# A hybrid attention, gated-recurrence and feed-forward layer in float32: score pairs issued together, the mark for values set later, the first gates and gated head fetched earlier

## The chip, the cores and the metric

The kernel runs on one core of a Trainium2 chip. The metric is the device time of one execution in microseconds, the median of several runs; a profiled execution of the same program gives the trace that is read here.

## The reference

One layer over 256 tokens of width 2048, all in float32:

```python
parts = x @ w_in                      # 9 parts of 1024 for three attention groups, then gq, gk, gv, gr, g_low, m_a, m_b
o, lse = _dilated_group(q, k, v, ...) # per group: windowed attention, 8 heads of 128, with a bias by distance
ya = softmax-over-groups(lse) * o, summed, @ w_proj_a
o  = _gla(gq, gk, gv, log_a)          # gated linear attention, 4 heads of 256 x 512, chunks of 64 tokens
yb = (normed(o) * silu(gr)) @ w_proj_b
y  = (sigmoid(m_a) * ya + sigmoid(m_b) * yb) @ w_out
x1 = layernorm(a * x + y)
f  = (silu(conv(x1 @ w_gate)) * (x1 @ w_up)) @ w_down      # 5632 wide, a 3-tap convolution over tokens
out = layernorm(a * x1 + f)
```

## The kernel before

**Numbers.** Each float32 operand is split into two parts (`split`, L138): ScalarE (ACT) copies it to a rounded high part `whi`, and VectorE (DVE) subtracts that from the original to leave a low part `wlo`. A product takes the matmuls high by high, high by low and low by high. Weights come as pieces of 128x1024 (512 KB), loaded by the SyncE queue into tiles `raw` or `quarter`, and each piece costs one split on ACT and one on DVE.

**Work in the first half.** The projections of x come in two forms. A *tile* (`b16`, L239) makes 128 columns with 32 matmuls; 64 of these make gq, gk and the attention's q and k. A *unit* (`seven`, L323) makes two 512-column blocks with seven products instead of eight (Strassen's scheme): its steps p1, p5, p6, p7, p3, p2, p4 appear in the trace as matmuls into the banks A, D, B, E, D, A, E, 24 matmuls each. Sums of x are kept in four resident tiles `comb`; sums of weights are made by DVE (L350) or by an accumulating DMA of GpSimd (POOL, L353). Ten units make v, gv, gr and most of m_a and m_b. `of_units` lists their steps, and the loop at L778 puts 56 tiles between them evenly.

**Side work.** Attention and the recurrence are cut into short closures in two lists, `side` and `slow`. `pump` (L188) runs one or two of them before every step and every tile. A closure may carry a mark and is held until the mark is in `passed`: the fetch of v (L515) waits for `values`, which the last `v` unit sets, and a stage of the recurrence waits for `gv`. Setting a mark (L754 to L756) was a step of its own in the list of units. Score matmuls (L470) of both token halves write into one PSUM bank, and DVE moves each half out (L472).

**Order.** The tracing order only sets priorities. A scheduler that builds the program decides, engine by engine, in which order the instructions stand, and `tc.issue_after(x)` keeps an instruction behind `x` on its engine. Each engine then works strictly in its order: an instruction that waits holds everything behind it, and that includes a DMA that stands in the ACT or POOL order and waits for its source.

**Around the middle.** After the units, two plain chunks of m_b (`m_t`, L798) are made, the early pool of SBUF tiles is closed and a late pool opens (L804). Then come four chunks `yp` (w_proj_a, 48 matmuls each, L899) and four chunks `pb` (w_proj_b, 96 each, L909). A chunk's gate is a spilled block of m, fetched again (tiles `m`, L876), put through a sigmoid (L884) and multiplied by DVE (L886). Beside the `yp` chunks the four heads of the recurrence's output are gated: `gated_get` fetches gr and o (L844), `gated_mul` takes the sigmoid and two products (L851 to L854), and `gated_turn` transposes the result on TensorE (`pt<-ident,sg`, L817; 8 transposes a head) and moves it out on ACT and DVE (`ob`, L824 and L825). The `pb` chunks read `ob`.

Of the kernel before, what the change touches and what calls it, by code (L numbers as in the profile page):

```python
# [11 lines left out]
F32 = mybir.dt.float32  # L12
# [5 lines left out]
P = 128  # L18
# [42 lines left out]
def hybrid_layer(ctx: ExitStack, tc: tile.TileContext, wp, xt, wgl, gw, par, relb, onehot, rows, xk, out):  # L61
# [73 lines left out]
    nc.gpsimd.memset(eps, EPS)  # L135


    def split(hi, lo, src):  # L138
        nc.scalar.activation(hi, src, AF.Copy)  # L139
        nc.vector.tensor_tensor(lo, src, hi.bitcast(F32), op=ALU.subtract)  # L140

    home = ["raw", 4]
# [306 lines left out]
    def attend(h, qk):  # L449
# [11 lines left out]
        def scores(g):  # L461
            def f():
                if not g:
                    st["s"] = blk("s0")[:, :384], big("s1", (768,))
                q, k = qk[g][:, :S], qk[g][:, S:]
                ps = bank("ps")
                for t in range(2):
                    n = (t + 1) * P
                    pt = ps[:, t * P : t * P + n]
                    nc.tensor.matmul(pt, q[:, t * P : (t + 1) * P], k[:, :n], start=True, stop=True)  # L470
                    s = st["s"][t][:, g * n : (g + 1) * n]
                    nc.vector.scalar_tensor_tensor(s, pt, scale, st["T"][:, g, S - n :], op0=ALU.mult, op1=ALU.add)  # L472
            return f
# [277 lines left out]
    def by_unit(name, n, sink, mark=None):  # L751
        for u in range(n):
            yield from seven(name, X, comb, AT[name, u], sink(u))
            if not u:  # L754
                yield lambda: passed.add("low")
        yield lambda: passed.add(mark)  # L756

    tiles = of_tiles()
    with tc.issue_after(loaded.ins):
# [12 lines left out]
        yield from by_unit("gr", 2, lambda u: to(GR, u))  # L772
        yield from by_unit("m", 3, lambda u: to(M[u // 2], u % 2))

    units = list(of_units())
    rest = list(tiles)
    done = 0
    for n, step in enumerate(units):  # L778
        pump()
        step()  # L780
        while done < (n + 1) * len(rest) / len(units):
            pump(2 if len(side) > 12 else 1)
            rest[done]()
            done += 1
# [8 lines left out]
        return f  # L793

    side.extend(ya_parts(h) for h in range(NH))
    yop = lambda kc: YA2[kc // 4][:, kc % 4]
    for n in range(2):
        pss = a_chunk("m", xop, 16, AT["mb"] + 8 * n, 3)  # L798
# [48 lines left out]
    def gated_mul(h):  # L847
        def f():
            sgs = [blk("sg") for _ in range(2)]
            for sg, (x, o) in zip(sgs, got[h]):  # L850
                nc.scalar.activation(sg, x, AF.Sigmoid)  # L851
                nc.vector.tensor_tensor(x, x, o, op=ALU.mult)
            for sg, (x, o) in zip(sgs, got[h]):
                nc.vector.tensor_tensor(sg, sg, x, op=ALU.mult)  # L854
            got[h] = sgs
        return f
# [6 lines left out]
    def both(*fs):  # L863
        def f():
            for g in fs:
                g()
        return f
# [28 lines left out]
    ya = []  # L896
    for n in range(4):
# [432 lines left out]
```

## Time and profile before

| | |
|---|---|
| median of 3 runs | 1888.59 us (1885.82 to 1895.8) |
| the profiled execution's own time | 1893.98 us |
| its span, first to last instruction | 1892.3 us |
| TensorE (PE) busy | 1824.9 us, 96% of the span, 8974 matmuls |
| weight loads (PEld) / DVE / ACT / POOL busy | 1523.2 / 1446.7 / 1088.3 / 243.5 us |
| granted TensorE clock, mean of the span | 0.989 |
| DMA | 478.53 MB, mean 253 GB/s |

A matmul's row in the trace lasts longer than its turn on the engine, because matmuls overlap: 24 matmuls of 128x512 that follow each other without a wait take 5.47 us, so one takes 0.228 us. PE's idle time is therefore the sum of the gaps that the view of waits names; it does not hold what a lower granted clock costs.

### The profile page before, as it was taken

To read this page: it belongs to the slowest core of one execution; us is meant where nothing else is said; L and a number is where in the kernel's file an instruction comes from. 1 tells how busy PE (TensorE), PEld (TensorE's weight loads), DVE (VectorE), ACT (ScalarE), POOL (GpSimd) and SP (SyncE) were. 2 spreads that over 40 slices of the span, in tenths; PEclk is the share of its full clock that TensorE was granted. 3 is DMA by queue.
4 is the path that set the end of the run, shared out by engine and by line. 5 is a ranking of instruction groups with operands and counts; after the bars stand their busy time and mean duration, and the time that the engine had idled before them with its cause. 6 is when DMAs were issued, how large, how long until landed. Compare 5 with 4: busy or idle time off the path is not lost.

```text
span 1892.3 us, 25421 instructions
## 1 busy us (share of the span) xinstructions
PE 1824.9 (96%) x8974; PEld 1523.2 (80%) x8974; DVE 1446.7 (76%) x1715; ACT 1088.3 (58%) x1400; POOL 243.5 (13%) x361
## 2 busy tenths in 40 slices
PE   8999998999999999999999999999999999999996
PEld 6877887788888888788778887888888888888785
DVE  6967997788797978865755556796597787877878
ACT  6655775565666666655654435665565556556553
POOL 0112111111111211111300001001011110110211
PEclk9999999999999999999999998999999999999998
DMA  8898987979889897896866518669679769779682
GB/s 303 278 304 228 305 276 218 326 211 306 256 260 338 216 310 241 258 338 229 301 235 205 189 60 321 210 166 321 225 206 341 241 202 338 222 229 341 190 276 95
DMA packets 145419, 478.53 MB, mean 253 GB/s; under 512 B 17649, under 2 KB 27916, under 8 KB 145292
## 3 DMA queue, kind: packets, MB, share of 16 engines
q1 hardware_dynamic: 96764, 345.09, 51.2%
q0 software_dynamic: 34416, 118.62, 25.5%
q10 hardware_dynamic: 14112, 13.21, 2.2%
q8 instruction: 70, 1.15, 0.2%
q14 instruction: 57, 0.47, 0.1%
HBM read 382.41 MB, written 32.67 MB: 219 GB/s over the span
## 4 chain that ended last, share of the span: by engine, by line
PE 69%; DMA 10%; DVE 9%; issue 4%; ACT 2%; POOL 1%; ACTq 0%; DVEq 0%; SPq 0%; POOLq 0%
PE qk L230 7%; DVE wlo L140 4%; PE wd_t L267 4%; PE wd_t L266 4%; PE wd_t L268 4%; PE qk L232 4%; PE fu L230 3%; PE fguE L337 3%; DMA quarter<-in_wp 3%; PE fg L230 3%; PE fguA L337 2%; DMA raw<-in_wp 2%; PE fguD L337 2%; PE mE L337 2%; PE pb_t L267 2%
## 5 line engine op out<-in xcount | busy, mean ns | idle before, releaser
L140 DVE TENSOR_TENSOR wlo<-quarter,whi 128x1024 fp32r<-128x1024 f32 x484 | 579.4, 1221 | 207.4 <-issue 61.1
L139 ACT ACTIVATE whi<-quarter 128x1024 fp32r<-128x1024 f32 x484 | 505.4, 1058 | 300.4 <-DVE quarter L350 58.5
L139 ACT ACTIVATE whi<-raw 128x1024 fp32r<-128x1024 f32 (+1 forms) x346 | 359.6, 1053 | 257.7 <-DMA raw<-in_wp 119.8
L140 DVE TENSOR_TENSOR wlo<-raw,whi 128x1024 fp32r<-128x1024 f32 (+1 forms) x346 | 414.4, 1215 | 112.8 <-ACT whi L139 49.6
L230 PE MATMUL qk<-x,whi 128*128 128x512 f32 x768 | 192.2, 399 | 0.0
L353 POOL DMA_DIRECT2D quarter<-quarter x120 | 105.6, 903 | 601.9 <-DMA quarter<-in_wp 157.1
L230 PEld LDWEIGHTS qk<-x,whi 128*128 128x128 f32 x768 | 141.9, 188 | 29.4 <-issue 1.4
L350 DVE TENSOR_TENSOR quarter<-quarter,quarter 128x1024 f32<-128x1024 f32 x120 | 143.2, 1219 | 0.3
L267 PE MATMUL wd_t<-wlo,h 128*128 128x512 f32 x352 | 137.6, 391 | 0.6 <-DVE wlo L140 0.6
L266 PE MATMUL wd_t<-whi,h 128*128 128x512 f32 x352 | 137.3, 392 | 0.0
L268 PE MATMUL wd_t<-whi,h 128*128 128x512 f32 x352 | 136.6, 389 | 0.0
L232 PEld LDWEIGHTS qk<-x,wlo 128*128 128x128 f32 x768 | 98.5, 191 | 7.5 <-DVE wlo L140 3.7
L232 PE MATMUL qk<-x,wlo 128*128 128x256 f32 x768 | 100.1, 283 | 3.3 <-DVE wlo L140 3.3
L230 PE MATMUL fu<-x,whi 128*128 128x512 f32 x368 | 88.0, 391 | 0.5 <-DVE gc L1004 0.4
L230 PE MATMUL fg<-x,whi 128*128 128x512 f32 x352 | 84.0, 390 | 0.0
L230 PEld LDWEIGHTS fu<-x,whi 128*128 128x128 f32 x368 | 68.2, 188 | 15.3 <-PE pt L1045 1.2
L267 PEld LDWEIGHTS wd_t<-wlo,h 128*128 128x128 f32 x352 | 66.2, 188 | 14.1 <-DVE wlo L140 1.3
L268 PEld LDWEIGHTS wd_t<-whi,h 128*128 128x128 f32 x352 | 66.1, 188 | 14.0 <-DVE h L140 0.3
L266 PEld LDWEIGHTS wd_t<-whi,h 128*128 128x128 f32 x352 | 66.0, 188 | 13.4 <-ACT h L139 0.3
L230 PEld LDWEIGHTS fg<-x,whi 128*128 128x128 f32 x352 | 65.5, 188 | 13.3
L230 PE MATMUL gqk<-x,whi 128*128 128x512 f32 x256 | 65.7, 409 | 4.4 <-ACT whi L139 3.6
L230 PEld LDWEIGHTS gqk<-x,whi 128*128 128x128 f32 x256 | 50.2, 200 | 17.8 <-ACT whi L139 7.4
(366 smaller groups left out, 3202.9 us busy)
## 6 DMA issues: line engine op xcount, KB each, us to landing
raw<-in_wp SPq DMA_DIRECT2D x342, 512.0 KB, 5.2
quarter<-in_wp SPq DMA_DIRECT2D x304, 512.0 KB, 6.9
quarter<-quarter POOLq DMA_DIRECT2D x120, 512.0 KB, 9.0
af<-acc POOLq DMA_DIRECT2D x32, 256.0 KB, 6.5
acc<-af POOLq DMA_DIRECT2D x28, 256.0 KB, 5.7
sp<-c POOLq DMA_DIRECT2D x14, 256.0 KB, 8.3
bias<-bvd ACTq DMA_DIRECT2D x32, 96.0 KB, 5.1
v<-vs ACTq DMA_DIRECT2D x24, 128.0 KB, 7.4
```

Of the source, the lines that this page charges most:

```text
L139: nc.scalar.activation(hi, src, AF.Copy)
L140: nc.vector.tensor_tensor(lo, src, hi.bitcast(F32), op=ALU.subtract)
L230: nc.tensor.matmul(ps, parts(kc)[0], opnd(kc), start=(kc == 0), stop=False)
L232: nc.tensor.matmul(ps[:, S:], parts(kc)[1], opnd(kc)[:, :S], start=False, stop=(kc == nk - 1))
L266: nc.tensor.matmul(ps, xh, hi, start=first, stop=False)
L267: nc.tensor.matmul(ps, xh, lo, start=False, stop=False)
L268: nc.tensor.matmul(ps, xl, hi, start=False, stop=last)
L337: nc.tensor.matmul(ps, a(kc)[which], w[:, k * 512 : (k + 1) * 512], start=(first and w is hi and which == 0 and kc == 0), stop=(w is lo an ...
L350: tt(a, a, b, op=ALU.add)
L353: nc.gpsimd.dma_start(a, b, accum_op=ALU.add)
```

## The change

It has five parts.

1. `scores` issues the matmuls of both token halves first and the two DVE instructions after them.
2. Setting a mark is no longer a step among the units. The mark is noted for two steps later and set there before `pump`. With that four empty steps leave the list (78 to 74), so the tiles and the side work shift against the units.
3. Two resident tiles `G01` and `GO` (of the size of a `comb` tile, from the same pool of 8) are fetched on the POOL queue while the `m_t` chunks are traced: the four blocks of the gates of chunks 0 and 1, and gr and o of head 0. Before, all of these were fetched from the late pool.
4. The sigmoids of gates and gated heads are kept behind the newest weight split on ACT.
5. The list of side work for the `yp` chunks starts with `mul(0)` and puts one of `mul` and `turn` at each of the eight places.

```diff
     def split(hi, lo, src):
-        nc.scalar.activation(hi, src, AF.Copy)
+        newest[:] = [nc.scalar.activation(hi, src, AF.Copy)]
...
                 for t in range(2):
                     n = (t + 1) * P
-                    pt = ps[:, t * P : t * P + n]
-                    nc.tensor.matmul(pt, q[:, t * P : (t + 1) * P], k[:, :n], start=True, stop=True)
+                    pts.append(ps[:, t * P : t * P + n])
+                    nc.tensor.matmul(pts[t], q[:, t * P : (t + 1) * P], k[:, :n], start=True, stop=True)
+                for t, pt in enumerate(pts):
+                    n = (t + 1) * P
                     s = st["s"][t][:, g * n : (g + 1) * n]
                     nc.vector.scalar_tensor_tensor(s, pt, scale, st["T"][:, g, S - n :], op0=ALU.mult, op1=ALU.add)
...
-        yield lambda: passed.add(mark)
+        yield mark
...
-    units = list(of_units())
+    units, marks = [], {}
+    for step in of_units():
+        if callable(step):
+            units.append(step)
+        else:
+            marks[len(units) + 2] = step
...
     for n, step in enumerate(units):
+        passed.add(marks.get(n))
         pump()
         step()
...
+    G01, GO = res("g01", F32), res("go", F32)
+
+    def first_fetches(t):
+        def f():
+            for n in range(2):
+                nc.gpsimd.dma_start(G01[:, 2 * n + t], M[0][n][t])
+            nc.gpsimd.dma_start(GO[:, 2 * t], GR[0][t])
+            nc.gpsimd.dma_start(GO[:, 2 * t + 1], O[0][t])
+        return f
+
+    slow.extend([first_fetches(0), first_fetches(1)])
...
-                nc.scalar.activation(sg, x, AF.Sigmoid)
+                with tc.issue_after(newest[0].ins):
+                    nc.scalar.activation(sg, x, AF.Sigmoid)
...
-                new = [fetch("m", M[br][n][t]) for t in range(2)]
+                if not br and n < 2:
+                    new = [G01[:, 2 * n + t] for t in range(2)]
+                else:
+                    new = [fetch("m", M[br][n][t]) for t in range(2)]
...
-            last_gate[:] = [nc.scalar.activation(x, x, AF.Sigmoid)]
+            with tc.issue_after(newest[0].ins):
+                last_gate[:] = [nc.scalar.activation(x, x, AF.Sigmoid)]
...
-    gated_get(0)()
+    got[0] = [[GO[:, 2 * t], GO[:, 2 * t + 1]] for t in range(2)]
     gated_get(1)()
...
     side.extend([
-        lambda: None, mul(0), both(turn(0), get(2)), mul(1),
-        both(turn(1), get(3)), mul(2), both(turn(2), mul(3)), turn(3),
+        mul(0), turn(0), both(mul(1), get(2)), turn(1),
+        both(mul(2), get(3)), turn(2), mul(3), turn(3),
     ])
```

The built program shows where this moves instructions. Line numbers of the change lie a little higher than those of before (L817 is L841, L139 and L140 are L141 and L142, L353 is L355, L518 is L523); numbers behind a name tell one buffer from another.

On PE, in the `yp` chunks, the transposes of head 0 stood so:

```order
L266 MATMUL yp_t_1089_8263<-whi_8330,ya_7729 128x512
L267 MATMUL yp_t_1089_8263<-wlo_8331,ya_7729 128x512
L268 MATMUL yp_t_1089_8263<-whi_8330,ya_7729 128x512
L817 MATMUL pt_8302<-ident,sg_8247 128x128
L817 MATMUL pt_8311<-ident,sg_8247 128x128
L266 MATMUL yp_t_1090_8264<-whi_8330,ya_7729 128x512
L817 MATMUL pt_8302<-ident,sg_8248 128x128
```

and now:

```order
L269 MATMUL yp_t_1074_8168<-wlo_8234,ya_7727 128x512
L270 MATMUL yp_t_1074_8168<-whi_8233,ya_7727 128x512
L268 MATMUL yp_t_1086_8276<-whi_8280,ya_7726 128x512
L841 MATMUL pt_8250<-ident,sg_8205 128x128
L841 MATMUL pt_8259<-ident,sg_8205 128x128
L269 MATMUL yp_t_1086_8276<-wlo_8281,ya_7726 128x512
L270 MATMUL yp_t_1086_8276<-whi_8280,ya_7726 128x512
L841 MATMUL pt_8250<-ident,sg_8206 128x128
```

They moved from behind 75 `yp` matmuls to behind 49. The four heads stood behind 75, 120, 168 and 192 `yp` matmuls and now stand behind 49, 96, 144 and 192.

On POOL, at the last unit of m, the four sums that p4 needs (`quarter<-quarter`, the second four) followed the first four at once:

```order
L353 DMA quarter_7130<-quarter_7243 128x1024
L353 DMA quarter_7132<-quarter_7245 128x1024
L353 DMA quarter_7134<-quarter_7247 128x1024
L353 DMA quarter_7077<-quarter_7515 128x1024
L353 DMA quarter_7079<-quarter_7517 128x1024
L353 DMA quarter_7081<-quarter_7519 128x1024
L353 DMA quarter_7083<-quarter_7521 128x1024
L112 DMA sp_7405<-c_963_7402 128x512
```

and now (`g` is G01, `go` is GO, `os` a spilled block of o):

```order
L355 DMA quarter_7166<-quarter_7301 128x1024
L814 DMA g_1007_7728<-sp_6168 128x512
...
L814 DMA g_1007_7728<-sp_5933 128x512
L112 DMA os_7222<-o_7216 128x512
L112 DMA os_7234<-o_7228 128x512
L815 DMA go_7729<-sp_4635 128x512
L816 DMA go_7729<-os_4516 128x512
L355 DMA quarter_7054<-quarter_7570 128x1024
L355 DMA quarter_7056<-quarter_7572 128x1024
```

Six fetches and two stores came between them. The first `g` reuses a `comb` tile that p7 of this unit reads, and the first `go` one that p3 reads.

On ACT, at the end of the third unit of v, the third fetch of v for head 0 stood so:

```order
L139 ACTIVATE whi_2769<-raw_2767 128x1024
L518 DMA v_2645<-vs_0_110 128x2x128
L258 ACTIVATE pa_2695<-qk_2661 128x256
L139 ACTIVATE whi_2825<-quarter_2704 128x1024
L496 ACTIVATE pT_2702<-ppt_2698 128x384
```

and now stands so:

```order
L141 ACTIVATE whi_2753<-raw_2751 128x1024
L523 DMA v_2895<-vs_0_110 128x2x128
L260 ACTIVATE pa_2691<-qk_2657 128x256
L141 ACTIVATE whi_2806<-quarter_2694 128x1024
L141 ACTIVATE whi_2816<-quarter_2696 128x1024
```

The fetch kept its place between the splits of a tile and the move `pa` of the tile before; what left the place is the attention's `pT` behind it. From the end of the `pb` chunks on, every engine's order is the same as before.

More of the change, by code (lines that the diff above doesn't have):

```diff
@@ L135, in hybrid_layer @@
     nc.gpsimd.memset(eps, EPS)
+    newest = []
     def split(hi, lo, src):
-        nc.scalar.activation(hi, src, AF.Copy)
+        newest[:] = [nc.scalar.activation(hi, src, AF.Copy)]
         nc.vector.tensor_tensor(lo, src, hi.bitcast(F32), op=ALU.subtract)
@@ L466, in f @@
                 ps = bank("ps")
+                pts = []
                 for t in range(2):
                     n = (t + 1) * P
-                    pt = ps[:, t * P : t * P + n]
-                    nc.tensor.matmul(pt, q[:, t * P : (t + 1) * P], k[:, :n], start=True, stop=True)
+                    pts.append(ps[:, t * P : t * P + n])
+                    nc.tensor.matmul(pts[t], q[:, t * P : (t + 1) * P], k[:, :n], start=True, stop=True)
+                for t, pt in enumerate(pts):
+                    n = (t + 1) * P
                     s = st["s"][t][:, g * n : (g + 1) * n]
```

## The prediction

> **What bounds the kernel now.** I read the page first, then PE's waits, then the stretches and the chain of waits where those waits lie.
>
> ```profile
> span 1892.3 us, 25421 instructions
> PE 1824.9 (96%) x8974; PEld 1523.2 (80%) x8974; DVE 1446.7 (76%) x1715; ACT 1088.3 (58%) x1400; POOL 243.5 (13%) x361
> ```
>
> PE is busy in 96% of the span and the change removes no matmul, so it can win only what PE loses: 1892.3 - 1824.9 = 67 us of idle time, and clock. The view of waits for PE says whom it waits for (total us, times, longest):
>
> ```profile
> PE pt L817 <- DVE ob L825: 4.6, 2, 3.0
> ...
> PE ps L470 <- DVE s L472: 3.7, 2, 2.6
> ...
> PE qk L232 <- DVE wlo L140: 3.3, 1, 3.3
> ...
> PE vD L337 <- DVE wlo L140: 3.0, 2, 2.6
> PE vE L337 <- ACT whi L139: 2.9, 2, 1.8
> PE pt L817 <- issue: 2.3, 1, 2.3
> PE vB L337 <- DVE wlo L140: 2.0, 1, 2.0
> PE mB L337 <- DVE wlo L140: 1.7, 2, 1.1
> ...
> PE gvB L337 <- DVE wlo L140: 1.5, 1, 1.5
> ...
> PE gvD L337 <- DVE wlo L140: 1.3, 1, 1.3
> PE yp_t L267 <- DVE wlo L140: 1.1, 1, 1.1
> ...
> PE pt L817 <- DVE sg L854: 1.1, 2, 0.9
> ```
>
> Nothing is large: the kernel loses its time in some thirty waits of 1 to 4 us. Three places belong to this change: the transposes of the gated heads with the yp row, the scores (ps), and the qk, gvD and gvB waits near 304 us, which a fetch of v causes.
>
> **The gated heads** (parts 3 to 5). The stretches of 10 us show busy times of PE, PEld, DVE, ACT and POOL, then the granted clock; the first is a full one. The chain of waits goes on behind the last gap:
>
> ```profile
> 895.00:905.00 10.00, 10.00 (x46) 8.28 (x45) 7.18 (x11) 6.53 (x12) 3.94 (x8) 1.00 0.84 269
> 905.00:915.00 10.00, 7.69 (x35) 5.97 (x33) 5.04 (x6) 4.68 (x5) 5.13 (x11) 1.00 1.01 383
> 925.00:935.00 10.00, 7.82 (x37) 5.94 (x37) 9.84 (x14) 6.48 (x12) 2.04 (x4) 1.00 0.84 258
> 945.00:955.00 10.00, 5.39 (x22) 4.17 (x21) 6.85 (x11) 6.16 (x11) 2.13 (x4) 0.81 0.83 290
> ...
> 953.17 0.43 PE pb_t L266
> ...
> 957.87 0.39 PE pb_t L268
> 958.26 0.24 PE pb_t L266
> ```
>
> Idle PE: 2.3 + 2.2 + 4.6 = 9.1 us, which the three pt rows and the yp row also make (4.6 + 2.3 + 1.1 + 1.1). Behind the last gap the clock falls to 0.81 and twelve matmuls, 953.17 to 958.26, take 5.1 us; at the later 0.228 us apiece they take 2.7. That is 2.4 us more, so this place costs 11.5 us.
>
> The Trainium skill, "TensorE: Matmul & The Clock Gate", Part 1: The HAM clock gate, says that the clock halves after an idle window of some 3.4 us and recovers after one busy window. The rows agree: gaps of 2.3 and 2.2 us left the clock at 1.00, 4.6 us did not, and 0.43 us is about twice 0.228. By the page alone the return would be half a window, 1.7 us (an estimate from the page), and the sum below 0.7 us smaller.
>
> Why PE waits there: the fetches of gr and o.
>
> ```profile
> 903.44 0.54 POOL L117 DMA_DIRECT2D gr<-sp  x1 [5.33 <-PE yp_t L268]
> ...
> 903.20 1.23 DVE L140 TENSOR_TENSOR wlo<-raw,whi 128x1024 fp32r<-128x1024 f32 x1 [0.77 <-issue]
> ...
> 910.70 0.69 DVE L852 TENSOR_TENSOR gr<-gr,o 128x512 f32<-128x512 f32 x1 [0.84 <-DMA o<-os]
> 913.08 0.69 DVE L852 TENSOR_TENSOR gr<-gr,o 128x512 f32<-128x512 f32 x1 [1.69 <-DMA o<-os]
> 913.69 1.29 DVE L854 TENSOR_TENSOR sg<-sg,gr 128x512 f32<-128x512 f32 x2
> ```
>
> The first can be issued at 903.4, the fourth block is used at 913.1, and DVE, nearly idle before that, then has all four heads' work in 30 us (9.84 of 10 busy in 925 to 935). In the change head 0's data and two chunks' gates lie ready, and DVE begins with head 0 after its fourth wlo. From the rows: that wlo ends at 903.2 + 1.2 = 904.4; two products gr by o (0.65 each, half of 1.29) and two with sg end at 907.0, the first pair's half at 906.4. PE reaches the transposes after 48 to 49 matmuls of 0.228 us from 895.0, at 906.1: 0.4 to 1 us late. Head 1's four blocks take the places in the queue that head 0's have in these rows, so DVE ends head 1 by about 915.1 (913.1 + 0.7 + 1.3), and the wlo behind it at 916.3; PE needs that wlo (85 `yp` matmuls and eight transposes of about 0.13 us after 895.0, plus the 0.5 us above) at 916 and head 1's transposes at 918.5. Heads 2 and 3 have 11 us each, and DVE's work for one chunk is four wlo, four products, two gates and four ob: 4.9 + 2.6 + 1.4 + 1.8 = 10.7 us. That just fits, so I keep 1.5 us of waits and no clock loss: 11.5 - 1.5 = **10.0 us won**. Bounds: 11.5 if nothing waits, 0 if DVE runs late again. The sigmoids moved behind weight splits cost ACT nothing new (58% busy); without that slack they delay a split by 0.6 us each.
>
> One step does go ahead of work on this path: ACT's table load and the first two sigmoids now stand around the last head's `ya`, whose way through DRAM and back ends here:
>
> ```profile
> 900.87 0.42 DVE L140 TENSOR_TENSOR ya<-yaf,ya 128x256 fp32r<-128x256 f32 x1
> ...
> 907.80 1.28 ACT L851 ACT_TABLE_LOAD   x1
> ```
>
> The load and one sigmoid (1.9 us) put that last split from 901.3 to 903.2 at most; PE wants it after 42 matmuls, at 904.6. Hidden by those matmuls: **0 us**, and under 2 us if the store lands that much later.
>
> **The moved fetches.** All eight are 256 KB on POOL's queue, six of them ahead of the second four weight sums of the last m unit. `go` waits until p3 has read its tile, and POOL holds the sums behind it.
>
> ```profile
> 815.87 5.47 PE mD L337 x24
> ...
> 833.70 5.49 PE mE L337 x24
> ...
> 816.83 0.86 POOL L353 DMA_DIRECT2D quarter<-quarter  x1 [2.63 <-ACT pa L258]
> ...
> quarter<-quarter POOLq DMA_DIRECT2D x120, 512.0 KB, 9.0
> ...
> DMA to landing us min/median/max: 4.6/9.0/20.2
> ```
>
> Before, the last of the four sums was issued at 816.8 and p4 (the last mE) began at 833.7. Now p3 (mD) ends at 821.3, two `go` issues take 1.1 us, and the four sums are issued from 822.4 to 825.1; with the median of 9.0 us they land from 831.4 to 834.1, and a split takes 2.3 us more. In the change a second qk tile of 5.5 us stands between p3 and p4, so p4 starts near 838 and wants its fourth piece 4.1 us later. First piece 4 us early, fourth 5 to 6 us: **0 us**, hidden by the two tiles. If the sum lands after the longest 20.2 us (700 to 817 us), the fourth is ready at 847.6 and PE stops for 5.5 us, and 8 with the clock's 2.4: the upper bound.
>
> **The scores** (part 1). The ps row is the second half's matmul waiting for DVE to read the first half out of the same bank. Issued together, it no longer waits: **3.7 us won**. DVE's instruction for the first half starts some 0.3 us later, beside other matmuls. Bounds: 0 to 3.7.
>
> **The later mark** (part 2).
>
> ```profile
> 290.92 0.72 POOL L563 DMA_DIRECT2D vs<-u  x1
> ...
> 300.55 0.53 ACTq L518 DMA_DIRECT2D v<-vs  x1
> 301.13 0.38 ACT L258 ACTIVATE pa<-qk 128x256 f32<-128x256 f32 x1 [9.28 <-PE qk L230]
> ...
> 301.54 0.42 DVE L259 TENSOR_TENSOR qk<-qk,pa 128x256 f32<-128x256 f32 x1 [7.77 <-ACT pa L258]
> 301.88 1.22 DVE L350 TENSOR_TENSOR quarter<-quarter,quarter 128x1024 f32<-128x1024 f32 x1
> 303.02 2.35 DVE L140 TENSOR_TENSOR wlo<-raw,whi 128x1024 fp32r<-128x1024 f32 x2
> ```
>
> The fetch of v stands in ACT's order and waits from 291.9 to 300.5 for the store of v to land. Behind it wait `pa`, on DVE the add after it, and the wlo that the qk row waits for; gvD and gvB pay the rest: 3.3 + 1.3 + 1.5 = 6.1 us. The later mark should remove that. The order says it does not: the scheduler pulls the fetch forward to the same place, ahead of the same `pa`. Only one weight sum of 1.2 us (L350) now stands behind the two wlo instead of ahead. **1.2 us won**, with bounds 0 and 6.1. The four steps that leave the list were empty and cost nothing; they shift side work. The vD, vE, vB and mB rows, 9.6 us, are splits that come late for such reasons: I count no change, and let them vary by half either way.
>
> **Sum.** 10.0 + 0 + 3.7 + 1.2 = 14.9 us. The profiled execution took 1893.98, so 1879.1 as it would be profiled; it lies 5.4 us above the median of the runs, 1888.59, and I take the win from that: 1888.59 - 14.9 = 1873.7, **1874 us**, 0.8% faster. About 0.5% (9.4 us) is what a measurement of this kernel can tell from no change, so the borders are 1879.1 and 1898.0.
>
> **Rivals.**
>
> *A, DVE becomes the bound of the yp stage.* For: 10.7 us of DVE work in a chunk of 10.9, and head 1's wlo within 0.3 us of its need. Against: DVE stood at 5.04 of 10 just before. If half of the 9.1 us returns and with it the clock's 2.4, 4.6 + 2.4 - 1.5 = 5.5 us come off the win: 1879 to 1880.
>
> *B, the queue of POOL.* The sums behind `go` land late, as priced, up to 8 us: 1874 to 1882.
>
> *C, the mark does what it says.* ACT is not held at 291.9, since the store lands earlier or the fetch finds it landed. For: the median landing of such stores is shorter than these 9.6 us. Against: the same place in the order. 6.1 - 1.2 = 4.9 us more: 1869.
>
> *D, slower.* One mechanism: with the empty steps gone, tiles and units meet in another order between 57 and 890 us, and the split of a piece stands behind another in-order wait on ACT or DVE (as near 291.9), so the waits of vD, vE, vB, mB and qk multiply. These rows, with gvB and gvD, hold 15.7 us. It eats the win when they double (1889) and is slower beyond 0.5% from about 2.6 times (+24 us, 1898). For: half of the order on all engines differs. Against: units and tiles have the same amount of loads and splits as before, and no row of the page shows an engine full there.
>
> **How the numbers follow.** The forecast (1866 to 1879) has 0.47, C 0.10, A 0.18, B 0.10, D 0.15. Faster by over 0.5%: nearly all of the forecast (0.44), C, a third of A and B's small stalls (0.05): 0.64, from which I take 0.04 because several small waits must all go. Slower: two thirds of D, 0.10. Same: the rest, 0.30. Range: from 1864 (the forecast with all upper bounds, 1.5 + 4.9 + 3 more than the sum) to 1892 (D where the rows double, and 3); the forecast's own is 1866 to 1879.
>
> **What would show it.** PE's waits on L470 gone; no wait above 1 us at the transposes of `sg` and a clock of 1.00 in every stretch of the yp and the first pb chunk (right), or DVE above 9.5 of 10 with waits on wlo there (A). Beside the last mE of the m units a wait for wlo with `quarter<-quarter` behind it (B). On ACT a fetch of v with some 9 us of nothing behind a store, once, near 290 (right about the mark), or none (C). The sum of PE's vD, vE, vB, mB and qk waits above 25 us would mean D. I am wrong in mechanism if the time falls and the yp stage still shows its 9.1 us.

## The result and the profile after

The changed kernel takes 1875.94 us (median of 4 runs, 1874.49 to 1877.26), the kernel before 1888.24 us (median of 4 beside it, 1885.82 to 1895.8). The ratio is 0.9928 with a 95% interval of 0.9899 to 0.9957: 0.7% faster. The forecast was 1874 us and faster. The sum came out; two of its terms were far off in opposite directions, as the runs below show, so that the sum came out is luck.

The page of the profiled execution (own time 1875.52 us) begins so, the span first, then each engine's busy time, share and instructions:

```profile
span 1873.8 us, 25413 instructions
PE 1819.0 (97%) x8974; PEld 1522.2 (81%) x8974; DVE 1443.2 (77%) x1715; ACT 1088.6 (58%) x1400; POOL 240.3 (13%) x361
```

The span is 18.5 us shorter than in the profile of before, 6 us more than the medians differ: that execution of before was 5.4 us above its median. PE's waits, those that answer to the rows quoted in the prediction (total us, times, longest):

```profile
PE vD L339 <- DVE wlo L142: 4.7, 2, 4.0
...
PE qk L234 <- DVE wlo L142: 3.3, 1, 3.3
PE vB L339 <- DVE wlo L142: 3.1, 2, 2.5
...
PE gvD L339 <- DVE wlo L142: 2.8, 2, 1.5
PE yp_t L269 <- DVE wlo L142: 2.4, 2, 1.2
...
PE pt L841 <- issue: 1.7, 1, 1.7
...
PE mB L339 <- DVE wlo L142: 0.5, 1, 0.5
```

The ps row is gone, as forecast, and the transposes of the heads wait 1.7 us in place of 8.0. But the rows vE (2.9) and gvB (1.5) are gone too, and mB fell from 1.7 to 0.5, none of which was forecast; the rows vD, vB and gvD rose by 1.1 to 1.7 each, and the yp row from 1.1 to 2.4.

The yp stage of the changed kernel in stretches of 10 us (columns as in the prediction: busy time of PE, PEld, DVE, ACT, POOL, granted clock, share of the DMA engines, GB/s):

```profile
893.00:903.00 10.00, 8.32 (x41) 6.70 (x40) 6.44 (x11) 6.50 (x12) 6.44 (x13) 1.00 0.81 304
903.00:913.00 10.00, 8.77 (x42) 6.97 (x42) 9.99 (x15) 2.51 (x4) 4.23 (x8) 1.00 0.99 358
913.00:923.00 10.00, 8.85 (x39) 7.01 (x38) 7.34 (x11) 7.55 (x12) 0.78 (x2) 1.00 0.77 263
```

The clock stays at 1.00, but PE still loses 1.7 + 1.2 + 1.2 = 4.1 us, and DVE is full for one stretch.

The instruction behind the fetch of v on ACT (start, duration, engine, instruction, idle time ahead of it and what ended that):

```profile
299.33 0.38 ACT L260 ACTIVATE pa<-qk 128x256 f32<-128x256 f32 x1 [8.67 <-DMA vs<-u]
```

The fetch, issued at 298.75 us, holds ACT for 8.7 us, as it did before (9.28 us).

Two stretches carry the rest of this text. One is the units and tiles with the plain gate chunks, from the first vA matmul to the first yp matmul; the other is the yp stage, from there to the first pb matmul. Both contain the same work in all kernels below. In the profiles of before and after, the first one reads:

```profile
57.27:895.00 837.73, 814.94 (x4076) 680.32 (x4075) 673.72 (x744) 510.64 (x644) 120.35 (x162) 1.00 0.87 271
```

```profile
56.96:883.72 826.76, 811.48 (x4077) 681.61 (x4076) 670.66 (x745) 514.28 (x648) 122.01 (x170) 1.00 0.88 277
```

and the yp stage:

```profile
895.00:952.83 57.83, 48.74 (x226) 39.35 (x224) 40.96 (x59) 37.31 (x61) 19.00 (x36) 0.99 0.89 306
```

```profile
883.72:935.64 51.92, 47.86 (x226) 39.00 (x224) 40.50 (x59) 31.84 (x52) 16.75 (x32) 1.00 0.87 313
```

So 11.0 us left the first stretch, 5.9 the second, 2.5 the pb chunks behind it (92.3 to 89.8 us, the clock), and the rest of the kernel took about 1 us more. The prediction had 4.9 for the first stretch and 10.0 for the other two.

### The profile page after: what moved, and what is told of

Read it like the earlier page. It is cut to its first block, busy times and chain, and to the rows that moved or that the text cites. A ratio compares the mean times of both kernels' runs of the same rounds, so it can differ in the third digit from the quotient of the medians.

```text
span 1873.8 us, 25413 instructions
## 1 busy us (share of the span) xinstructions
PE 1819.0 (97%) x8974; PEld 1522.2 (81%) x8974; DVE 1443.2 (77%) x1715; ACT 1088.6 (58%) x1400; POOL 240.3 (13%) x361
## 4 chain that ended last, share of the span: by engine, by line
PE 74%; DVE 8%; DMA 5%; issue 2%; ACT 2%; POOL 0%; ACTq 0%; DVEq 0%; SPq 0%; POOLq 0%
PE qk L232 8%; PE qk L234 4%; DVE wlo L142 4%; PE wd_t L269 4%; PE wd_t L270 4%; PE wd_t L268 4%; PE fg L232 3%; PE fguE L339 3%; PE fu L232 3%; DMA raw<-in_wp 3%; PE fguA L339 2%; PE fguD L339 2%; PE mA L339 2%; PE mD L339 2%; PE mE L339 2%
## 5 line engine op out<-in xcount | busy, mean ns | idle before, releaser
L142 DVE TENSOR_TENSOR wlo<-quarter,whi 128x1024 fp32r<-128x1024 f32 x484 | 578.9, 1220 | 215.0 <-issue 57.3
L141 ACT ACTIVATE whi<-quarter 128x1024 fp32r<-128x1024 f32 x484 | 505.8, 1057 | 288.8 <-DVE quarter L352 71.0
L141 ACT ACTIVATE whi<-raw 128x1024 fp32r<-128x1024 f32 (+1 forms) x346 | 359.3, 1052 | 248.4 <-DMA raw<-in_wp 129.5
L142 DVE TENSOR_TENSOR wlo<-raw,whi 128x1024 fp32r<-128x1024 f32 (+1 forms) x346 | 413.9, 1214 | 101.4 <-ACT whi L141 52.5
L355 POOL DMA_DIRECT2D quarter<-quarter x120 | 105.1, 899 | 642.5 <-DMA quarter<-in_wp 161.1
L232 PEld LDWEIGHTS qk<-x,whi 128*128 128x128 f32 x768 | 143.0, 188 | 30.3 <-issue 1.4
```

The costliest lines, as they stand in the source:

```text
L141: newest[:] = [nc.scalar.activation(hi, src, AF.Copy)]
L232: nc.tensor.matmul(ps, parts(kc)[0], opnd(kc), start=(kc == 0), stop=False)
L355: nc.gpsimd.dma_start(a, b, accum_op=ALU.add)
```

## The experiments

Theory T, formed from these two profiles: 8 us of the win are from the gated heads, 3.7 from the scores and nothing from the marks, and what the first stretch shows beyond that belongs to one long execution of before. Its main rival, R: the new order of units and tiles won it. All runs in one table; the stretches are those of each kernel's profiled execution. The median of before differs between sittings (1888 to 1891 us; the three sittings of the experiments ran on three different chips), so the ratio to the runs of before beside each kernel is the better column.

| kernel | median us (runs) | ratio, 95% interval | units and tiles us | yp stage us |
|---|---|---|---|---|
| before | 1888.24 (4) | | 837.7 | 57.8 |
| before, a second profile | 1889.67 (1) | | 836.6 | 55.2 |
| changed | 1875.94 (4) | 0.9928, 0.9899 to 0.9957 | 826.8 | 51.9 |
| before + scores | 1886.52 (12) | 0.9971, 0.9958 to 0.9983 | 833.2 | 55.6 |
| before + heads | 1885.28 (12) | 0.9968, 0.9955 to 0.9981 | 836.6 | 52.0 |
| before + marks | 1883.38 (7) | 0.9961, 0.9945 to 0.9977 | 829.5 | 57.8 |
| before + fewer steps | 1883.26 (12) | 0.9968, 0.9956 to 0.9981 | 826.4 | 58.4 |
| before + late mark | 1888.55 (12) | 0.9996, 0.9985 to 1.0008 | 833.7 | 56.4 |
| changed, old score code | 1877.49 (6) | 0.9944, 0.9927 to 0.9961 | 829.5 | 50.8 |
| changed, no early fetch | 1881.01 (12) | 0.9964, 0.9950 to 0.9977 | 827.1 | 55.8 |
| changed, free sigmoids | 1876.69 (6) | 0.9920, 0.9900 to 0.9939 | 826.6 | 53.7 |
| changed, old side list | 1871.62 (5) | 0.9893, 0.9873 to 0.9913 | 827.2 | 47.1 |
| changed + v late | 1869.60 (4) | 0.9889, 0.9869 to 0.9909 | 818.9 | 51.0 |
| the same + low-rank split late | 1866.74 (5) | 0.9876, 0.9853 to 0.9899 | 820.3 | 51.7 |

### Each part alone

**Scores.** On the kernel before, only this:

```diff
-                    pt = ps[:, t * P : t * P + n]
-                    nc.tensor.matmul(pt, ...)
+                    pts.append(ps[:, t * P : t * P + n])
+                    nc.tensor.matmul(pts[t], ...)
+                for t, pt in enumerate(pts):
+                    n = (t + 1) * P
```

> The kernel before with part 1 alone: the two score matmuls of a pair are issued ahead of the two DVE instructions that read them. Theory T (the change's 12.3 us are some 8 from the gated heads, 3.7 from the scores and nothing from the marks): PE's waits on ps, 3.7 us before, are gone and nothing takes their place; the order of work elsewhere stays nearly the same, so the time falls by 3 to 4 us (ratio about 0.998). Rival S: the second half's wait was hidden by a split that came late anyway, and PE now waits at the next instruction: no change, within 1 us. Rival R (the win of the change comes from the order in which units and tiles meet): also about nothing, with waits of splits that move by 1 to 2 us either way.

Measured: 1886.52 us against 1889.93 of before in the same sitting, 3.4 us by the medians, or 0.29% (5.5 us) by the ratio. There is no ps row among PE's waits. The stretch of units and tiles is shorter by 3.5 to 4.6 us than in the two profiles of before:

```profile
59.68:892.84 833.16, 814.43 (x4077) 682.84 (x4075) 670.53 (x743) 510.74 (x645) 120.22 (x162) 0.99 0.87 272
```

The term of 3.7 us fits this edit alone, and rival S falls.

**Heads.** Parts 3 to 5 of the change on the kernel before (`G01`, `GO` and `first_fetches`, the two `issue_after(newest[0].ins)`, the new side list).

> The kernel before with parts 3 to 5 alone: the first two chunks' gates and head 0's data fetched beside the plain gate chunks, sigmoids behind weight splits, the side list rearranged. PE's order up to the plain gate chunks is that of before, instruction by instruction. Theory T: the yp stage falls from 57.8 to about 52 us and the first matmuls of pb run at full clock (2.5 us more), so 8 to 8.5 us off the median of the kernel before (ratio about 0.9955); and since the first 845 us have the order of before, they show how much of the 845.5 us that the profile of before spent there belonged to that one execution: about 5 us, so some 840 here. Rival R: those 5 to 11 us come from the new order of units and tiles; then m_t begins at 845 here too, and the heads are worth 8 at most, of which some is given back behind pb.

Measured: 4.7 us faster by the medians (1885.28 against 1889.93), 0.32% or 6.0 us by the ratio. The stage is as short as in the changed kernel, though some of it ran at half clock; the stretch ahead of it, with the order of before, is as long as before. The rows of the two stretches, the yp stage first:

```profile
893.73:945.69 51.96, 49.37 (x226) 40.53 (x224) 40.61 (x59) 31.99 (x52) 16.73 (x32) 0.97 0.93 322
```

```profile
57.18:893.73 836.55, 816.23 (x4077) 681.64 (x4076) 672.11 (x743) 512.60 (x647) 124.75 (x170) 0.99 0.87 274
```

So theory T is wrong on the first stretch: the same order takes 836.6 us here and 837.7 in the profile of before. The changed kernel's 826.8 is not luck of one execution: 10 us of the difference come from parts 1 and 2. And the heads are worth less than the 8 us that T gave them.

**Marks.** Part 2 on the kernel before.

> The kernel before with part 2 alone: 74 steps in place of 78, each mark two steps later. Theory T: the fetch of v is still held on ACT near 290 us and PE still loses about 6 us there; the other waits of splits change place and not their sum: within 2 us of before (ratio 0.999 to 1.001). Rival C (the mark does what it says): 5 to 6 us faster. Rival R (the new order of units and tiles is where the change won): 5 to 7 us faster with the 6 us near 290 still there, from waits of gv, v and m tiles that are gone.

Measured: 6.5 us faster (1883.38 against 1889.93), 0.39% by the ratio, and the fetch of v is held as before:

```profile
300.90 0.38 ACT L258 ACTIVATE pa<-qk 128x256 f32<-128x256 f32 x1 [8.72 <-DMA vs<-u]
```

Rival R is right, and rival C wrong: the marks win by something else than the mark. Among PE's waits between 57 and 895 us the vE and gvB rows are gone, and most of the ps row, which the score edit was to remove:

```profile
PE vD L337 <- DVE wlo L140: 4.0, 1, 4.0
PE qk L232 <- DVE wlo L140: 3.6, 1, 3.6
PE vB L337 <- DVE wlo L140: 3.1, 2, 2.5
PE gvD L337 <- DVE wlo L140: 1.3, 1, 1.3
...
PE ps L470 <- DVE s L472: 0.7, 2, 0.5
```

### Which half of the marks

Part 2 does two things: four empty steps leave the list, and a mark is set two steps later. Each alone, on the kernel before. Fewer steps, as a difference from part 2:

```diff
-            marks[len(units) + 2] = step
+            marks[len(units)] = step
```

and the late mark, with the empty step kept:

```diff
+            units.append(lambda: None)
             marks[len(units) + 2] = step
```

> Part 2 alone as in the run of marks alone (1883.4 us, 6.5 below the kernel before on this chip), but each mark is set right after its unit, as before, and only the four empty steps are gone: 74 steps in place of 78. Theory K (what the marks won came from the empty steps: each unit step now draws 1/74 of the tiles and not 1/78, so tiles meet other pieces): the win stays, 5 to 7 us, and the vE waits near 125 us (2.9 us before) are gone, since no mark is due that early. Rival L (the marks' later place wins it): within 1.5 us of the kernel before.

> The other half of part 2 alone: the empty steps stay (78 steps), and each mark is set two steps later. Theory K: within 1.5 us of the kernel before, with the vE waits near 125 us still there and the fetch of v still held until about 300 us. Rival L: 5 to 7 us faster. If each half wins 2 to 4 us, both theories are half right.

Measured: fewer steps 1883.26 us, the late mark 1888.55, against 1888.66 of before beside them. Theory K holds: the empty steps are the whole of it, the mark's place is worth nothing that these runs can tell (0.9996, 0.9985 to 1.0008). PE's waits of the first between 57 and 895 us, three of its four largest rows:

```profile
PE vD L337 <- DVE wlo L140: 4.2, 2, 3.9
...
PE gvD L337 <- DVE wlo L140: 2.5, 2, 1.5
PE ps L470 <- DVE s L472: 2.3, 3, 1.6
```

and of the second, which has the vE and gvB rows of before:

```profile
PE vE L337 <- ACT whi L139: 3.2, 2, 1.8
...
PE gvB L337 <- DVE wlo L140: 1.8, 1, 1.8
```

The loop hands out tiles by `(n + 1) * len(rest) / len(units)`; with 74 in place of 78 every tile meets other pieces of its unit. Two waits of vE near 125 us, long before any mark that a value waits for, go with it. Which split stands behind which instruction at each place was not worked out, so why 74 is better than 78 stays open; nothing in these runs says that fewer is better in general.

### Do the parts add up?

Alone they gave 0.29 + 0.32 + 0.39 = 1.0% by the ratios, together 0.72%. The intervals of the four ratios, 0.12 to 0.29% to either side, are wide enough for a difference of 0.28%, so an overlap is not shown by the sum. One possible overlap was tested: the changed kernel with the score code of before.

> The changed kernel without part 1: each score matmul again followed by the DVE instruction that reads it. With part 2 alone PE's waits on ps were 0.7 us, against 3.7 before. Theory O (part 2's order had already taken that wait, so the scores' term and the marks' term overlap): within 1 us of the changed kernel, 1875 to 1877, with ps waits below 1 us. Rival P (the terms are independent, and the wait comes back with the old code): 3 to 4 us slower than the changed kernel, 1879 to 1880.

Measured: 1877.49 us, 1.6 us above the changed kernel by the medians, 0.16% (3.0 us) by the ratios, whose intervals overlap. What is left of the waits on ps there is a quarter of before:

```profile
PE ps L472 <- DVE s L474: 0.9, 3, 0.5
```

The waits are as theory O has them, below 1 us; the time lies between O and P, and its interval excludes neither. With part 2 most of those waits are gone in any case (0.7 us alone). In the one profile of each half it is the late mark that moves them, and not the empty steps: no ps row with the late mark, 2.3 us with fewer steps. Beside part 2 the score edit is worth some 1.6 to 3.0 us, or nothing that these runs can tell.

### What made the yp stage shorter

**Without the early fetch** the two resident tiles are gone; sigmoids and list stay as changed.

```diff
-    slow.extend([first_fetches(0), first_fetches(1)])
...
-                if not br and n < 2:
-                    new = [G01[:, 2 * n + t] for t in range(2)]
...
-    got[0] = [[GO[:, 2 * t], GO[:, 2 * t + 1]] for t in range(2)]
+    gated_get(0)()
```

> The changed kernel without the two resident tiles: the first two chunks' gates and head 0's data are fetched where they were before, while the sigmoids stay behind weight splits and the side list keeps its new order. Theory F (the late fetches of gr and o made the idle time, the rest of parts 4 and 5 only keeps ACT and DVE in step): the yp stage goes back from 51.9 to 56 to 58 us and some matmuls run at half clock, 4 to 6 us slower than the changed kernel, 1880 to 1882; with head 0's products now one place earlier in the list, it may be 1 to 2 us more. Rival G (the list and the sigmoids' place made it): the stage stays below 53.5 us and the time within 1.5 us of the changed kernel.

Measured: 1881.01 us, 5.1 above the changed kernel. The stage takes 55.8 us, with a gap of 4.0 us at head 0's transposes and half clock behind it. The row of the stage, and that of PE's waits:

```profile
885.97:941.81 55.84, 50.23 (x226) 40.94 (x224) 40.75 (x59) 33.91 (x54) 18.21 (x34) 0.94 0.84 296
```

```profile
PE pt L828 <- issue: 4.0, 1, 4.0
```

Theory F holds.

**With free sigmoids** (the two `issue_after` of part 4 taken out):

> The changed kernel without part 4: the sigmoids of the gates and of the gated heads are free to stand anywhere in ACT's order. PE's order stays the same, instruction by instruction. Theory F (the early fetches are what shortened the yp stage): the stage stays at 51 to 53 us and the time within 1.5 us of the changed kernel. Rival H (without the pins a sigmoid that waits for a late fetch holds weight splits on ACT, as the fetch of v does near 300 us): a gap of 1 to 3 us before a matmul that wants whi, 2 to 4 us slower, 1878 to 1880.

Measured: 1876.69 us, 0.8 above the changed kernel; the stage took 53.7 us in its one profile. Part 4 is worth nothing that these runs can tell.

**With the side list of before** (part 5 undone):

```diff
-        mul(0), turn(0), both(mul(1), get(2)), turn(1),
-        both(mul(2), get(3)), turn(2), mul(3), turn(3),
+        lambda: None, mul(0), both(turn(0), get(2)), mul(1),
+        both(turn(1), get(3)), mul(2), both(turn(2), mul(3)), turn(3),
```

> The changed kernel with the side list of before: an empty place first, then products and transposes in the old order, each head's transposes one place later than now. Theory F: head 0's data lie ready and every product has more time, so the 1.7 us gap at head 0's transposes goes; the later heads' work collects at the end, where pb wants it, and up to 2 us come back there: within 1.5 us of the changed kernel. Rival J (the new list is needed to keep DVE in step): DVE above 9.5 of 10 busy in the last 20 us of the stage and 3 us or more of idle PE at its end, 3 to 5 us slower, 1879 to 1881.

Measured: 1871.62 us, 4.3 us *below* the changed kernel; both theories expected no gain. In the profile PE does not wait once in the stage:

```profile
884.93:931.99 47.06, 47.06 (x226) 39.20 (x224) 38.78 (x57) 31.25 (x52) 16.74 (x32) 1.00 0.91 326
```

The new list costs 51.92 - 47.06 = 4.9 us (the four other profiles with it, the early fetches and part 4 take 50.8 to 52.0 us). Of this 1.7 us are the gap at head 0's transposes, which now come before the products are ready, and 1.2 and 1.2 us are waits for a `wlo`; 0.8 us lie in PE's busy time (47.86 against 47.06). DVE's order tells where the first wait for a `wlo` comes from. In the changed kernel, from the last product of the first gates on:

```profile
897.08 1.28 DVE L915 TENSOR_TENSOR g<-g,yp_t 128x512 f32<-128x512 f32 x2
901.92 0.88 DVE L849 SCALAR_TENSOR_TENSOR ob<-pt,prm,ob 128x256 fp32r<-128x256 f32 x2 [3.56 <-ACT ob L848]
...
905.90 3.49 DVE L142 TENSOR_TENSOR wlo<-raw,whi 128x1024 fp32r<-128x1024 f32 x3
```

and with the list of before:

```profile
898.15 1.28 DVE L915 TENSOR_TENSOR g<-g,yp_t 128x512 f32<-128x512 f32 x2
899.34 1.23 DVE L142 TENSOR_TENSOR wlo<-raw,whi 128x1024 fp32r<-128x1024 f32 x1
```

With head 0's transposes one place earlier, DVE comes to `ob` of head 0 at 898.4, before ACT has done its half, stands there for 3.6 us, and does head 1's products next; the weight splits are queued behind both and start at 905.9, where PE waits for the first. With the old list a split is done at 899.3, in that hole. ACT is late with its half because it stands too: ahead of `ob` in its order comes head 1's sigmoid, which waits 3.1 us for the fetch of gr:

```profile
899.94 0.63 ACT L876 ACTIVATE sg<-gr 128x512 f32<-128x512 f32 x1 [3.09 <-DMA gr<-sp]
...
901.43 0.82 ACT L848 ACTIVATE ob<-pt,prm 128x256 fp32r<-128x256 f32 x2
```

So the hole goes back to an instruction that waits for a late DMA, as at the fetch of v. The second wait for a `wlo`, at 916.6 us, stands behind a hole of 2.7 us at head 1's `ob`; ACT had stood 5.0 us for a weight piece ahead of its own. The time of DVE's work was not the trouble (40.5 of 51.9 us): in the kernel with the list of before DVE is full for 10 us as well, and PE does not wait.

```profile
910.00:920.00 10.00, 10.00 (x50) 8.38 (x49) 10.00 (x14) 7.31 (x11) 2.46 (x5) 1.00 0.96 353
```

**A second profile of before**, the kernel unchanged, to see how far one execution speaks for the others:

> The kernel before, unchanged, for a second profiled execution of the same order of work. Theory Q (the profiled execution that the prediction was made from was a bad one in the yp stage: other profiles with the same order there show 145.5 to 148.3 us from the first yp matmul to the first of wo, it shows 150.1): here that stretch takes 145 to 148.5 us, and its gaps sum to less than 9.1 us or the first matmuls of pb run at full clock. Rival (that order of work always loses so much): 149.5 us or more, with a clock below 0.9 behind the last gap.

The yp stage in it:

```profile
895.71:950.92 55.21, 50.93 (x226) 40.97 (x224) 40.59 (x59) 37.04 (x59) 18.92 (x36) 0.94 0.86 306
```

The stage took 55.2 us, and pb behind it ran at full clock: with it, 145.1 us to the first wo matmul, against 150.1 in the profile that the prediction used. Theory Q holds. Over the six profiles with the old fetches and the old list (57.8, 55.2, 55.6, 57.8, 58.4, 56.4) the stage takes 56.9 us in the mean. All six lost clock: the first one mostly behind the stage, in pb, the other five inside it (a granted clock of 0.91 to 0.97 over the stage); over the five with the change's heads (51.9, 52.0, 51.0, 50.8, 51.7) it takes 51.5, and one of them lost clock (0.97).

### The wait that the change leaves

The changed kernel with the fetch of v kept behind the newest weight split in ACT's order:

```diff
-                nc.scalar.dma_start(st["v"][:, g], src)
+                with tc.issue_after(newest[0].ins):
+                    nc.scalar.dma_start(st["v"][:, g], src)
```

> The changed kernel with one more edit: each of the three fetches of v of a head is kept, in ACT's order, behind the newest weight split at the place where the program issues it. In the changed kernel ACT stands at the third fetch until 298.75 us, 8.7 us idle before the next instruction, and PE loses 3.4, 1.4 and 1.7 us at 301 to 310 us. Theory V (that fetch alone is the cause): ACT is not idle for longer than 2 us there, the three gaps go, and the time falls by 6 to 6.5 us below the changed kernel's, to about 1869.5. Rival W (the splits of that stretch come late for another reason as well, such as the weight sums that they read): half or less is won, 0 to 3 us. Rival U (the fetch later is late for the head that wants v, whose mixing matmuls then wait): no win or a loss of 1 to 3 us.

Measured: 1869.60 us, 6.3 below the changed kernel, as theory V had it. ACT around the fetch now:

```profile
296.95 2.05 ACTq L524 DMA_DIRECT2D v<-vs  x2
299.05 0.39 ACT L260 ACTIVATE pa<-qk 128x256 f32<-128x256 f32 x1 [1.06 <-PE qk L234]
```

The same 40 us of the changed kernel, then of this one:

```profile
280.00:320.00 40.00, 33.96 (x169) 27.89 (x168) 31.05 (x30) 21.17 (x26) 4.56 (x6) 1.00 0.82 250
```

```profile
280.00:320.00 40.00, 40.00 (x202) 34.04 (x201) 38.05 (x37) 25.84 (x29) 5.76 (x7) 1.00 0.91 272
```

PE was idle for 6.0 us there and is not idle any more. One fetch, standing in order ahead of splits that had nothing to do with it, cost 6.3 us by the medians (0.39%, or 7.4 us, by the ratios).

The same thought at a second place: near 136 us ACT loads the low-rank weights and stands at their split. On top of the edit above, that split became a step of its own, two turns later:

```diff
-        split(glh, gll, glr)
...
+    def low_splits():
+        start_mask()
+        with tc.issue_after(newest[0].ins):
+            split(*low["parts"], low["raw"])
...
-        slow.extend([("low", low_loads), start_mask, low_rank, low_parts, *gla_gates])
+        slow.extend([("low", low_loads), low_splits, low_rank, low_parts, *gla_gates])
```

> The kernel with the late fetch of v (1869.6 us) and one more edit of the same kind at another place: near 136 us there, ACT issues the load of the low-rank weights (glr) and stands at their split until they land, 7.8 us idle, and PE then waits 4.2 us for a weight split behind it. Here the loads stay where they are and the splits of what they bring become a step of their own, two turns of the side list later, behind the newest weight split. Theory V (what costs time is an instruction in ACT's order that waits for a DMA just issued): the 4.2 us gap at 145.9 us goes, some 4 us faster than the kernel with the late fetch of v, 1865 to 1866. Rival X (the weight splits there are late for their sums as well): 1 us or less is won.

Measured: 1866.74 us, but its interval (0.9853 to 0.9899) and that of the kernel below it (0.9869 to 0.9909) overlap widely, and in its profile the gap of PE is still there (4.0 us near 149 us, on vD as before). The wait moved instead of going. On ACT no other instruction stands any more between the six loads of the low-rank gates:

```profile
140.22 7.04 ACTq L592 DMA_DIRECT2D gws<-in_gw  x6
147.31 0.60 ACT L365 ACTIVATE s<-vA 128x512 f32<-128x512 f32 x1 [9.46 <-DMA gws<-in_gw]
```

Five of the six are issued by 143.0 us, the last at 146.94, and ACT stands until then. The chain of waits puts that last issue down to the landing of a weight piece at 146.92 us (`raw<-in_wp`, under way since 131.02); why a load of the low-rank gates waits for it is not shown. The expectation of 4 us missed; whether this version is faster than the one with the late fetch alone is open. It and the late fetch are the fastest that ran, 0.5% and 0.3% below the changed kernel. The late fetch of v together with the old side list was not run; from their rows, 1869.60 and 51.04 - 47.06 = 4.0 us less in the stage, it would stand near 1866 us, an estimate.

## Why the prediction was right, and where it was wrong

The time lies 2 us from the forecast and well within its own range. Two terms were off in opposite directions, and the sum hides it: the time was right by luck.

**The gated heads, 10.0 us: mis-sized, some 5.4 measured.** The mechanism stands: late fetches of gr and o made the gaps, and the early ones take 56.9 - 51.5 = 5.4 us out of the stage. Both ends of "11.5 - 1.5" were off. The 11.5 was read from one execution; against the 47.06 us of a stage without any wait, the six profiles with the old order lose 56.9 - 47.1 = 9.8 in the mean, most of them with the clock's loss inside it. The 1.5 that I kept became 51.5 - 47.1 = 4.4. The step that failed is "That just fits, so I keep 1.5 us of waits": it added up DVE's work (10.7 us in a chunk; 40.5 in four chunks measured) and did not ask in which order ACT and DVE stand at it. Rival A was half right for that reason. Its sign showed, 9.99 of 10 in 903 to 913 us with a wait on wlo there, and the transposes waited 1.7 us where I wanted no wait above 1. But the waits came through holes in DVE's order and not through a full DVE, which the list of before has too, and without loss of clock. With that list nothing waits, as in the upper bound, and the early fetches are worth 9.8 us in the stage (by its one profile), not 11.5.

**Part 5 was counted as free.** It loses about 4.9 us in the stage; I had put the transposes at "0.4 to 1 us late" (1.7 measured) and not looked at what stands behind `ob` on DVE.

**The moved fetches, 0: right, but not as I had it.** No row of PE's waits beside the last m unit names a split of those sums; rival B falls. I had `go` wait for p3 and the four sums behind it issued from 822.4 us. In the trace the first `g` waited for p5 (`mD`) and the first `go` for p6 (`mB`), not for p7 and p3, and the sums were issued from 795.4 to 805.6, over 20 us before p4 began at 828.0:

```profile
793.84 0.54 POOL L815 DMA_DIRECT2D go<-sp  x1 [7.69 <-PE mB L339]
```

**The scores, 3.7: right alone, less beside part 2** (1.6 to 3.0 us, not clear of noise). Two edits reach the same wait.

**The later mark, 1.2: nothing that can be told.** That the scheduler pulls the fetch back to its place was right, and rival C falls: the three gaps at 301 to 310 us are as large as before. The one weight sum of 1.2 us that I counted is within the interval of the late mark's run and does not show. What rival C priced at 6.1 us is real, and the late fetch of v wins it.

**"The four steps that leave the list were empty and cost nothing": the step that failed most.** They win 5 to 7 us alone. I had named the mechanism as rival D (tiles and units meet in another order, and the vE, vB, mB, gvB waits move) and gave it one sign: slower. It went the other way: vE and gvB gone, mB down by 1.2, vD, vB and gvD up by 1.1 to 1.7 each. "I count no change, and let them vary by half either way" allowed 4.8 of 9.6 us; the stretch of units and tiles gave 11.0 where the scores' 3.7 and the mark's 1.2 were forecast. The rows just named account for only 1.3 us of that. All waits in the stretch together fell by 7.5 us (837.73 - 814.94 = 22.8 to 826.76 - 811.48 = 15.3), 3.7 of them on ps and 2.2 on the recurrence's pgo, which the prediction did not look at. The other 3.5 us are in PE's busy time, with the granted clock at 1.00 in both rows; where they come from was not found.

In all: heads 5 to 6, scores 1.6 to 3, empty steps 5 to 7, against 12.3 by the medians.

## What to carry to other kernels

On an engine that works in order, look for the instruction that waits for a DMA landing (a fetch of what was just stored, a split of what was just loaded) and count what is queued behind it: moving one such fetch on ACT behind the next weight split was worth 6.3 us, half as much as the whole change. Where code deals work out by a count of steps, an empty step is not free, and its effect is an order to be tried, not a sum to be worked out. Before a stage's loss becomes a term, see it in a second profile; and a rearranged list deserves its own run, since one of the five parts here took back 4.9 us of what another had won.

## What the runs showed of the hardware

The clock does not follow the length of a gap alone. Ahead of the same transposes, a gap of 1.7 us left the clock at 1.00 in the changed kernel (the stretch from 893 us above), and gaps of 1.66 and 0.26 us halved it in the kernel with the heads alone. Its PE rows:

```profile
906.43 0.30 PE L832 MATMUL pt<-ident,sg 128*128 128x128 f32 x1 [1.66 <-issue]
906.99 1.73 PE L832 MATMUL pt<-ident,sg 128*128 128x128 f32 x7 [0.26 <-DVE sg L870]
908.37 0.77 PE L268 MATMUL yp_t<-whi,ya 128*128 128x512 f32 x1
```

From 906.99 the seven transposes stand 0.21 us apart and the matmuls 0.43, until about 910.5: 3.5 us at half speed, some 1.7 us lost. In the second profile of before, gaps of 1.8, 0.2 and 1.1 us within 4.7 us, with eight transposes and one matmul between them, halved it for a dozen matmuls; in the first profile one gap of 2.3 us, and 2.2 us in three gaps, did not. The 4.6 us that the prediction set beside a window of 3.4 us are two gaps, the longer one 3.0 us.

The Trainium skill, "TensorE: Matmul & The Clock Gate", Part 1: The HAM clock gate, says that the activity window is about 3.4 us long and free-running, so that the point of change depends on where in the window the work falls. The traces agree: in the granted clock of each of the fourteen profiles the spells at half speed begin on one raster of 3.41 us and, but for the one that runs into the end of the kernel, last one, two or three of its steps. The rule that the prediction took from that section, a window idle throughout, does not hold here, and the measurement decides. Here are two steps of the raster in the kernel with the heads alone, then in the changed kernel, then three in the second profile of before (the second and third in one row):

```profile
903.41:906.82 3.41, 1.66 (x7) 0.92 (x6) 2.39 (x4) 2.03 (x4) 3.27 (x7) 1.00 0.81 280
906.82:910.24 3.42, 3.25 (x12) 2.87 (x13) 1.90 (x4) 1.86 (x3) 1.90 (x4) 0.53 1.02 375
```

```profile
893.70:897.11 3.41, 1.73 (x9) 1.21 (x8) 3.41 (x6) 2.93 (x5) 3.41 (x7) 1.00 0.77 274
897.11:900.52 3.41, 3.41 (x19) 2.86 (x18) 1.25 (x3) 0.58 (x2) 1.62 (x4) 1.00 0.85 321
```

```profile
925.75:929.16 3.41, 1.52 (x9) 1.04 (x9) 3.35 (x7) 3.41 (x7) 1.48 (x4) 1.00 0.59 183
929.16:935.99 6.83, 5.72 (x14) 4.52 (x15) 6.80 (x9) 4.34 (x9) 0.49 (x1) 0.51 0.89 318
```

PE is idle for 1.75, 1.68 and 1.89 us in the first step of each, and the clock behind it is halved, whole and halved. Over all fourteen profiles the border lies there, near half a step: of 73 full-speed steps with more than 1.9 us of idle PE behind the first 60 us all were followed by one at half speed, of some 7200 with less than 1.7 us one was, and of the 16 in between 11. A gap of 2.3 us that an edge of the raster divides (1.5 us in the step from 910.26 in the first profile of before) leaves the clock alone. A step at half speed costs up to 1.7 us, half its length. Where the raster lies changes from one execution to the next (a step begins at 128.61 us in the first profile of before and at 130.44 in the second), so for a forecast a gap of 1.8 to 3.5 us (an estimate: from half a step to a whole one) carries a chance of such a loss and not a yes or no.
